# A two-layer hybrid decoder: the gate norm's root from ScalarE's table, first operands of a K block on VectorE, three sums ahead of the token sum

## Chip, core and metric

The kernel runs on one core of a Trainium2 chip. The metric is the device time of one execution in microseconds (us). The engines are called PE (TensorE, the matrix engine), DVE (VectorE), ACT (ScalarE), POOL (GpSimd) and SP (SyncE, which here issues the loads).

## What is computed

A trunk of two layers on 256 tokens of width 2048, in float32. Layer 0 mixes tokens by gated linear attention (GLA), layer 1 by attention with a forget gate (FoX); each mixer is followed by a gated MLP with a short convolution. Each half layer is normed and modulated by vectors that come from the condition c by one large product with w_mod.

```python
cond = jax.nn.silu(c)
for i in range(DEPTH):
    mod = (cond @ w_mod[i] + b_mod[i])[:, None, :]
    sh_m, sc_m, g_m, sh_f, sc_f, g_f = jnp.split(mod, 6, axis=-1)
    h = rmsnorm(x, norm_mix[i]) * (1.0 + sc_m) + sh_m
    ...                                   # gla_mixer or fox_mixer
    x = x + (1.0 + g_m) * y
    h = rmsnorm(x, norm_ffn[i]) * (1.0 + sc_f) + sh_f
    x = x + (1.0 + g_f) * conv_ffn(h, ...)
return rmsnorm(x, norm_final)

def gla_mixer(h, w_in, w_gate, b_gate, g_norm, w_out):
    q, k, v, r, a = split(h @ w_in)       # 1024, 1024, 2048, 2048, 16 columns
    ...                                   # chunked linear attention, 4 heads of 512
    o = rmsnorm(o, g_norm)                # for each head: the gate's norm
    return (o * silu(r)) @ w_out
```

## The kernel before

**Products.** Activations lie turned (128 features by 256 tokens), in 16 K tiles. Each float32 operand is split in a high and a low part: a weight tile `w` (128x1024, 512 KB) is cast by ACT to `wh` (L125), and DVE forms `wl` = w - wh (L129); the activation `h` has a high part from ACT (L528) and a low part from DVE (L533). A product takes three matmuls: high by high (L621), wh by the low part of h (L622), wl by the high part (L623). One weight tile against one K tile is 8 outputs by 3 matmuls of 128x256; such a step is a "use" of a weight.

**The start.** The scale and shift of the first four K tiles come from eight "early sums" on PE (L1270): eight tiles of w_mod of 1 MB, four matmuls each. ACT copies a finished row (`er`, L1276), PE turns it into columns (L1279) and DVE adds the bias (L1283). Ahead of them PE turns x (L441), and the token sum (L483) gives the norm's root. Between the later sums stand KEEP matmuls on a constant tile (L1308), whose output nobody reads.

**K blocks.** The rest of the modulation of layer 0 isn't there when the first weights are. So w_in is worked in three blocks of K tiles, 0 to 3, 4 to 8 and 9 to 15 (STARTS), and within each over the pieces q, k, v0, v1, r0, r1 (1024 columns each) and a (16). A piece's sums are copied out at the end of a block (L750) and put back into PSUM at the next (L609, `preload`). Meanwhile the w_mod products of the next block run on DVE as multiply-adds into `acc` (L273, L275; tiles `wm`), a certain number per use (`pace["bg"]`); at a column group's end DVE transposes and reduces (L285, L286), PE sums over quadrants (L302), and DVE adds the bias (L318). At a block's last use but one the queue is emptied (`drain_bg`), and at the block's start `h` for its first K tile is made (`hooks`). In `make_h` DVE multiplies x by the root (L527), ACT makes the high part (L528), then the scaled and shifted value is made again in float32, for K tiles 0 to 2 on DVE (L530), for others on ACT (L532), and DVE subtracts (L533).

**The gate's norm.** In the last block the attention runs as a side queue of steps, let out at `pace["side"]` steps per use. Its last steps: `apply` (per head; leaves the sums of squares in `pvar`, L916), `scale_of` (the reciprocal root `grs` for two heads by shift, constant and three Newton steps on DVE, L403 to L416), `normalise` (DVE puts a root on a diagonal `dg`, L422; PE spreads it, L424; DVE multiplies `oT`, L927), `open_gate` (silu on ACT, L942; product on DVE, L944). `raw_operand` then splits oT for w_out (L548, L549).

**Order.** The program is recorded in the order of the code and then put in order by a scheduler with a model of times; `tc.issue_after` pins an instruction behind another. DMA loads go out on SP's queue one after another (L248), and each waits there for its buffer.

## Time and profile before

| | |
|---|---|
| median of 3 runs | 2445.66 us (2445.61 to 2447.43) |
| the profiled execution | 2444.97 us, span 2443.3 us |
| mean granted PE clock | 0.989 |
| busy: PE, DVE, ACT, POOL | 98%, 78%, 54%, 1% of the span |
| DMA | 638.31 MB, 261 GB/s over the span |

Times in the rows of the profile are counted from the first instruction of the span. "[idle before <-releaser]" at a row's end is how long the engine did nothing ahead of it, and what ended that. A row with "x4" joins neighbours of one kind; "PEld" is the load of a stationary operand, which overlaps PE. The granted clock is 1.00 at full rate. A matmul's duration in a row is that of its way through the array, and the next one starts earlier.

### The profile page before, as it was taken

To read this page: it belongs to the slowest core of one execution; us is meant where nothing else is said; L and a number is where in the kernel's file an instruction comes from. 1 tells how busy PE (TensorE), PEld (TensorE's weight loads), DVE (VectorE), ACT (ScalarE), POOL (GpSimd) and SP (SyncE) were. 2 spreads that over 40 slices of the span, in tenths; PEclk is the share of its full clock that TensorE was granted. 3 is DMA by queue.
4 is the path that set the end of the run, shared out by engine and by line. 5 is a ranking of instruction groups with operands and counts; after the bars stand their busy time and mean duration, and the time that the engine had idled before them with its cause. 6 is when DMAs were issued, how large, how long until landed. Compare 5 with 4: busy or idle time off the path is not lost.

```text
span 2443.3 us, 46907 instructions
## 1 busy us (share of the span) xinstructions
PE 2388.1 (98%) x19089; PEld 2292.1 (94%) x19093; DVE 1901.7 (78%) x2548; ACT 1326.6 (54%) x1819; POOL 16.1 (1%) x35
## 2 busy tenths in 40 slices
PE   7999998999999999999999999999999999999998
PEld 5898898999999999999988888999999999999998
DVE  5887878887689999987577998887776777777544
ACT  4666864544656556543464555554755555555433
POOL 0000000000000000000000000000000000000000
PEclk9999998999999999999999999999999999999999
DMA  9997877899668999899589887686777777756553
GB/s 377 328 338 240 288 249 274 288 322 322 181 191 278 314 302 313 315 327 322 168 291 314 298 288 244 210 300 234 232 232 234 234 233 235 232 193 220 192 190 104
DMA packets 188293, 638.31 MB, mean 261 GB/s; under 512 B 23849, under 2 KB 24859, under 8 KB 187692
## 3 DMA queue, kind: packets, MB, share of 16 engines
q1 hardware_dynamic: 187112, 634.12, 77.2%
q8 instruction: 149, 2.44, 0.4%
q10 hardware_dynamic: 964, 1.20, 0.1%
q14 instruction: 68, 0.56, 0.1%
HBM read 633.14 MB, written 2.10 MB: 260 GB/s over the span
## 4 chain that ended last, share of the span: by engine, by line
PE 95%; DVE 2%; ACT 2%; DMA 1%; issue 1%; SPq 0%; DVEq 0%; ACTq 0%
PE pa L622 25%; PE pa L623 25%; PE pa L621 25%; PE pa L668 5%; PE pa L669 5%; PE pa L667 5%; DVE wl L129 1%; DMA wm<-in_w_mod_dram 1%; PE pe L1270 0%; DVE acc L275 0%; ACT wh L125 0%; PE pm L483 0%; PE pm L877 0%; DMA xtok<-in_x_dram 0%; PE pm L1088 0%
## 5 line engine op out<-in xcount | busy, mean ns | idle before, releaser
L125 ACT CAST wh<-w 128x1024 fp32r<-128x1024 f32 x820 | 857.4, 1048 | 965.7 <-PE pa L622 735.3
L129 DVE TENSOR_TENSOR wl<-w,wh 128x1024 fp32r<-128x1024 f32 x820 | 996.5, 1217 | 438.8 <-ACT wh L125 428.6
L622 PE MATMUL pa<-h,wh 128*128 128x256 f32 x3584 | 993.7, 278 | 13.3 <-DVE h L533 13.3
L621 PE MATMUL pa<-h,wh 128*128 128x256 f32 x3584 | 991.6, 278 | 2.2 <-ACT h L528 1.3
L623 PE MATMUL pa<-h,wl 128*128 128x256 f32 x3584 | 991.0, 278 | 1.7 <-DVE wl L129 1.7
L622 PEld LDWEIGHTS pa<-h,wh 128*128 128x128 f32 x3584 | 677.4, 189 | 15.1 <-DVE h L533 14.8
L621 PEld LDWEIGHTS pa<-h,wh 128*128 128x128 f32 x3584 | 675.3, 189 | 5.4 <-issue 1.5
L623 PEld LDWEIGHTS pa<-h,wl 128*128 128x128 f32 x3584 | 675.6, 189 | 2.0 <-DVE wl L129 1.9
L622 PE MATMUL pa<-op,wh 128*128 128x256 f32 x1920 | 529.4, 277 | 1.8 <-DVE op L549 1.8
L621 PE MATMUL pa<-op,wh 128*128 128x256 f32 x1920 | 528.9, 278 | 0.4 <-ACT op L548 0.2
L623 PE MATMUL pa<-op,wl 128*128 128x256 f32 x1920 | 524.8, 277 | 0.0
L275 DVE SCALAR_TENSOR_TENSOR acc<-wm,cT,acc 128x1024 f32<-128x1024 f32 (+2 forms) x360 | 444.3, 1235 | 10.7 <-DMA wm<-in_w_mod_dram 9.4
L622 PEld LDWEIGHTS pa<-op,wh 128*128 128x128 f32 x1920 | 362.0, 189 | 2.3 <-DVE op L549 2.3
L621 PEld LDWEIGHTS pa<-op,wh 128*128 128x128 f32 x1920 | 361.2, 189 | 1.1 <-ACT r L750 0.6
L623 PEld LDWEIGHTS pa<-op,wl 128*128 128x128 f32 x1920 | 359.2, 189 | 0.0
L668 PE MATMUL pa<-wh,h 128*128 128x512 f32 x512 | 200.2, 392 | 0.0
L667 PE MATMUL pa<-wh,h 128*128 128x512 f32 x512 | 198.8, 391 | 0.0
L669 PE MATMUL pa<-wl,h 128*128 128x512 f32 x512 | 194.4, 392 | 0.0
L669 PEld LDWEIGHTS pa<-wl,h 128*128 128x128 f32 x512 | 96.0, 188 | 19.7 <-DVE wl L129 0.3
L667 PEld LDWEIGHTS pa<-wh,h 128*128 128x128 f32 x512 | 96.1, 188 | 19.4
L668 PEld LDWEIGHTS pa<-wh,h 128*128 128x128 f32 x512 | 96.1, 188 | 19.2
L1140 ACT ACTIVATE y<-u,cw 128x256 f32<-128x256 f32 x176 | 101.6, 599 | 6.7 <-DVE act L1156 4.1
(264 smaller groups left out, 1351.3 us busy)
## 6 DMA issues: line engine op xcount, KB each, us to landing
wm<-in_w_mod_dram SPq DMA_DIRECT2D x320, 512.0 KB, 5.2
w<-in_ffn_w_up_dram SPq DMA_DIRECT2D x320, 512.0 KB, 4.5
w<-in_ffn_w_down_dram SPq DMA_DIRECT2D x176, 512.0 KB, 4.5
w<-in_fox_w_in_dram SPq DMA_DIRECT2D x128, 512.0 KB, 5.1
w<-in_gla_w_in_dram SPq DMA_DIRECT2D x96, 512.0 KB, 5.8
w<-in_gla_w_out_dram SPq DMA_DIRECT2D x32, 512.0 KB, 5.9
w<-in_ffn_w_up_dram SPq DMA_DIRECT2D x64, 256.0 KB, 4.0
w<-in_fox_w_out_dram SPq DMA_DIRECT2D x32, 512.0 KB, 5.9
```

The costliest lines, as they stand in the source:

```text
L125: nc.scalar.copy(out=hi, in_=src)
L129: order["v"] = nc.vector.tensor_tensor(out=lo, in0=src, in1=hi.bitcast(F32), op=ALU.subtract).ins
L275: nc.vector.scalar_tensor_tensor(out=st["a"], in0=wt[:, j, :], scalar=col, in1=st["a"], op0=ALU.mult, op1=ALU.add)
L621: nc.tensor.matmul(o, wh[:, ms], rh, start=(first and m % 2 == 0), stop=False, skip_group_check=True)
L622: nc.tensor.matmul(o, wh[:, ms], rl, start=False, stop=False, skip_group_check=True)
L623: nc.tensor.matmul(o, wl[:, ms], rh, start=False, stop=last, skip_group_check=True)
L667: nc.tensor.matmul(o, lh[:, ts_], wh[:, hs_], start=first, stop=False, skip_group_check=True)
L668: nc.tensor.matmul(o, ll[:, ts_], wh[:, hs_], start=False, stop=False, skip_group_check=True)
L669: nc.tensor.matmul(o, lh[:, ts_], wl[:, hs_], start=False, stop=last, skip_group_check=True)
L1140: nc.scalar.activation(y, u, AF.Identity, scale=cw[:, l * 3 + 2, r:r + 1], bias=cw[:, 6 + l, r:r + 1])
```

## The change

- `scale_of` uses `table_root`: DVE scales (L498 of the changed kernel), ACT takes the reciprocal root from its table (L506), and one third-order step on DVE mends it (L507 to L509). `scale_of(0)` runs before the end of piece v1, `scale_of(2)` before r0, and the norms of heads 2 and 3 go behind the first gate's steps. The pace of the side queue is 0.9 and then 1.2 steps a use for 0.8 and 1.4.
- In `make_h` the affine step for the first four K tiles of a block (of tiles 1 to 4 elsewhere) is on DVE. A new mark `fresh["h"]` makes the next use run `by_part`: all high by high products, then all with the low part, then all with wl. It is set when h of a block's first K tile is made.
- At the start three early sums stand ahead of the token sum (`first_sums`); KEEP is 3 for 5; the second weight's split is recorded ahead of h's second tile.
- `staged_h` queues the w_mod products for blocks 1 and 2 at once at the very start, at a pace worked out for each, and forces at a block's start only what that block needs; the hooks that make h sit one use earlier. Depth of prefetch and the constants SLOAD and NEAR of the loader change.

```diff
-SLOAD = 48
+SLOAD = 100
-NEAR = 20
+NEAR = 50
-KEEP = 5
+KEEP = 3
-GP0 = 0.8
-GP1 = 1.4
+GP0 = 0.9
+GP1 = 1.2
-EASE, N5 = 3, 5
+N5 = 5
+MARKS = (4, 9, 16)
+EASE = (4, 5)
+EARLY = 3
...
-        prefetch(PEND)
+        prefetch(min(PEND, fetched["use"] // 2 + 1))
...
-    def load_x(xs):
+    def load_x(xs, between):
...
         half_sum()
-        token_sum(ss["t"][:, 0, :], True, True)
+        with tc.issue_after(between()):
+            token_sum(ss["t"][:, 0, :], True, True)
...
+    def table_root(q, src, scale):
+        v = tmp.tile([P, 16], F32, tag="rs_v", name=nm("rv"))[:, :4]
+        nc.vector.tensor_scalar(out=v, in0=src, scalar1=scale, scalar2=None, op0=ALU.mult)
+        root_step(q, v, tmp.tile([P, 16], F32, tag="rs_t", name=nm("rt"))[:, :4])
+
     def token_rstd(q, n_):
-
-        order["r"] = nc.scalar.activation(q, ss["p"][:, :n_], AF.Abs_reciprocal_sqrt, bias=epsc).ins
-        t = t1("ra")[:, :n_]
-        nc.vector.scalar_tensor_tensor(out=t, in0=ss["p"][:, :n_], scalar=EPS, in1=q, op0=ALU.add, op1=ALU.mult)
+        root_step(q, ss["p"][:, :n_], t1("ra")[:, :n_])
+
+    def root_step(q, src, t):
+
+        order["r"] = nc.scalar.activation(q, src, AF.Abs_reciprocal_sqrt, bias=epsc).ins
+        nc.vector.scalar_tensor_tensor(out=t, in0=src, scalar=EPS, in1=q, op0=ALU.add, op1=ALU.mult)
         nc.vector.scalar_tensor_tensor(out=t, in0=t, scalar=-0.5, in1=q, op0=ALU.mult, op1=ALU.mult)
         nc.vector.scalar_tensor_tensor(out=q, in0=t, scalar=1.5, in1=q, op0=ALU.add, op1=ALU.mult)
 
@@ -526,11 +539,23 @@
...
-            if m < 3:
-                nc.vector.tensor_scalar(out=t, in0=t, scalar1=sc, scalar2=sh, op0=ALU.mult, op1=ALU.add)
-            else:
-                nc.scalar.activation(t, t, AF.Identity, scale=sc, bias=sh)
+            with ExitStack() as es:
+                if m == 1 and order["w"] is not None:
+                    es.enter_context(tc.issue_after(order["w"]))
+                    order["w"] = None
+                if m - (max(b for b in STARTS if b <= m) if (l, kind) == (0, "m") else 1) < 4:
+                    nc.vector.tensor_scalar(out=t, in0=t, scalar1=sc, scalar2=sh, op0=ALU.mult, op1=ALU.add)
+                else:
+                    nc.scalar.activation(t, t, AF.Identity, scale=sc, bias=sh)
             ins = nc.vector.tensor_tensor(out=lo, in0=t, in1=hi.bitcast(F32), op=ALU.subtract).ins
+            if m == 0 and (l, kind) == (0, "m"):
+                with tc.issue_after(ins):
+                    split_to(1, 2)
+                    with tc.issue_after(hot):
+                        split_to(2, 2)
+                order["w"] = order["v"]
+            if m == 0 or (l, kind) == (0, "m") and m in STARTS:
+                fresh["h"] = True
...
+        def mms(m, k, wh, wl, rh, rl, n_=None):
             first, last = base is None and k == kts[0], k == kts[-1]
             ms = slice(m * P, (m + 1) * P)
             o = ps[m // 2][:, m % 2, :]
-            nc.tensor.matmul(o, wh[:, ms], rh, start=(first and m % 2 == 0), stop=False, skip_group_check=True)
-            nc.tensor.matmul(o, wh[:, ms], rl, start=False, stop=False, skip_group_check=True)
-            nc.tensor.matmul(o, wl[:, ms], rh, start=False, stop=last, skip_group_check=True)
+            for i, (w_, r_) in enumerate(((wh, rh), (wh, rl), (wl, rh))):
+                if n_ is None or n_ == i:
+                    mm = nc.tensor.matmul(o, w_[:, ms], r_, start=(first and i == 0 and m % 2 == 0),
+                                          stop=last and i == 2, skip_group_check=True)
+            return mm.ins
+
+        def by_part(ms, args):
+            edge = None
+            for n_ in range(3):
+                with ExitStack() as es:
+                    if edge is not None:
+                        es.enter_context(tc.issue_after(edge))
+                    for m in ms:
+                        last_ = mms(m, *args, n_)
+                    edge = last_
...
-                for args in held if k == kts[1] else ():
+                if k == kts[1] and fresh["h"]:
+                    fresh["h"] = False
+                    by_part(range(4), held[0])
                     for m in range(4):
-                        mms(m, *args)
+                        mms(m, *held[1])
+                elif k == kts[1]:
+                    for args in held:
+                        for m in range(4):
+                            mms(m, *args)
                 while k == kts[1] and held:
                     args = held.pop(0)
                     for m in range(4, 8):
                         mms(m, *args)
+            elif fresh["h"]:
+                fresh["h"] = False
+                by_part(range(8), (k, wh, wl, rh, rl))
...
-            return lambda: rsqrt(grs[:, 2 * hd:2 * hd + 4], pvar[:, 2 * hd:2 * hd + 4], 1.0 / 512.0, 4)
+            return lambda: table_root(grs[:, 2 * hd:2 * hd + 4], pvar[:, 2 * hd:2 * hd + 4], 1.0 / 512.0)
...
-        side.extend((apply(0), scores(2), apply(1), scores(3)))
+        side.extend((apply(0), scores(2), apply(1), scores(3), scale_of(0)))
         fold("v1", piece("v1", kts, off["v1"]))
         drain_side()
-        side.extend((apply(2), apply(3), scale_of(0), scale_of(2), normalise(0), normalise(1), normalise(2), normalise(3)))
+        side.extend((apply(2), apply(3), normalise(0), normalise(1), scale_of(2)))
         pace["side"], pace["sacc"] = GP0, 0.0
...
         side.extend(open_gate(0, b) for b in range(4))
+        side.extend((normalise(2), normalise(3)))
...
+    def first_sums():
+        with tc.issue_after(order["x"]):
+            for args in todo[:EARLY]:
+                last_ = early_sum(*args)
+        return last_
+
+    load_x(xs, first_sums)
     with tc.issue_after(order["s"]):
         turn_rows()
     first_h = make_h(0, "m")
     for i, args in enumerate(todo):
         if i + WIDE < len(todo):
             early_load(*todo[i + WIDE])
+        if i < EARLY:
+            continue
...
+    need = {}
+
     def staged_h(m):
-        if m in STARTS[:-2]:
-            n_ = STARTS.index(m) + 1
-            for key in ("sc_m", "sh_m"):
-                queue(mod_tasks(0, key, STARTS[n_] * P, BLOCKS[n_] * P, wide=True))
-            n_use = 6 * BLOCKS[n_ - 1]
-            set_pace(n_use - EASE)
-            end = fetched["use"] + n_use + (m > 0)
-            hooks[end - 1] = drain_bg
-            hooks[end] = lambda: h(STARTS[n_])
+        if m == 0:
+            for m0, m1 in zip(MARKS, MARKS[1:]):
+                for key in ("sc_m", "sh_m"):
+                    queue(mod_tasks(0, key, m0 * P, (m1 - m0) * P, wide=True))
+                need[m0] = len(bg)
+            pace["bg"] = need[MARKS[0]] / float(6 * BLOCKS[0] - EASE[0])
+            hooks[6 * MARKS[0] - 1] = lambda: h(MARKS[0])
+            hooks[6 * MARKS[1]] = lambda: h(MARKS[1])
+        elif m == MARKS[0]:
+            pace["bg"], pace["acc"] = len(bg + pending) / float(6 * BLOCKS[1] - EASE[1]), 0.0
+        if m in need:
+            while steps_done[0] < need[m]:
+                bg_step()
+            flush_resting(True)
         return first_h(m)
 
-    h = lazy(staged_h, KT, 2, STARTS)
+    h = lazy(staged_h, KT, 2, MARKS)
```

How the order of instructions moves, at three places. PE at the start, from behind the turning of x, before (wm are tiles of w_mod, ss the squares summed over tokens, rows and brow small vectors that are turned):

```order
L483 MATMUL pm_219<-ss_153,onesD 128x256
L206 MATMUL pm_221<-ident,rows_106 128x98
L1270 MATMUL pe_237<-wm_139,cz_120 32x512 x4
L1270 MATMUL pe_237<-wm_141,cz_120 32x512 x4
L1270 MATMUL pe_237<-wm_143,cz_120 32x512 x4
L1270 MATMUL pe_237<-wm_145,cz_120 32x512 x3
L211 MATMUL pm_225<-ident,brow_127 128x96
L1270 MATMUL pe_237<-wm_145,cz_120 32x512
L1270 MATMUL pe_269<-wm_235,cz_120 32x512 x3
```

and after:

```order
L1318 MATMUL pe_219<-wm_139,cz_120 32x512 x4
L1318 MATMUL pe_219<-wm_141,cz_120 32x512 x4
L1318 MATMUL pe_219<-wm_143,cz_120 32x512 x4
L489 MATMUL pm_232<-ss_153,onesD 128x256
L209 MATMUL pm_234<-ident,rows_106 128x98
L1318 MATMUL pe_219<-wm_145,cz_120 32x512 x4
L214 MATMUL pm_238<-ident,brow_127 128x96
L1327 MATMUL pm_262<-ones,er_260 128x1 x4
L1318 MATMUL pe_269<-wm_248,cz_120 32x512 x4
```

Three sums moved ahead of the token sum (L483 before, L489 after), and the first row's turn (L1327) stands ahead of the fifth sum.

ACT at the start of block 1 (h is the operand of K tile 4 and on, r the last piece's sums that are copied out, w the weight tiles), before:

```order
L125 CAST wh_1064<-w_987 128x1024
L125 CAST wh_1100<-w_989 128x1024
L125 CAST wh_1152<-w_991 128x1024
L528 ACTIVATE h_1128<-hn_1129,mod 128x256
L528 ACTIVATE h_1128<-hn_1134,mod 128x256
L528 ACTIVATE h_1128<-hn_1139,mod 128x256
L750 COPY r_197_1144<-pa_980 128x512
L750 COPY r_197_1144<-pa_981 128x512
L750 COPY r_197_1144<-pa_982 128x512
L750 COPY r_197_1144<-pa_983 128x512
L528 ACTIVATE h_1128<-hn_1191,mod 128x256
L125 CAST wh_1181<-w_993 128x1024
```

and after:

```order
L128 CAST wh_994<-w_941 128x1024
L128 CAST wh_1026<-w_991 128x176
L541 ACTIVATE h_1097<-hn_1098,mod 128x256
L541 ACTIVATE h_1097<-hn_1103,mod 128x256
L541 ACTIVATE h_1097<-hn_1108,mod 128x256
L797 COPY r_199_1145<-pa_987 128x512
L797 COPY r_199_1145<-pa_988 128x512
L128 CAST wh_1065<-w_1024 128x1024
L797 COPY r_199_1145<-pa_989 128x512
L797 COPY r_199_1145<-pa_990 128x512
L541 ACTIVATE h_1097<-hn_1188,mod 128x256
L128 CAST wh_1115<-w_1063 128x1024
```

Before, the casts of the block's first weights (wh_1064 and wh_1100 for its first pair) stood ahead of the operands; after, the pair's casts (wh_1065 and wh_1115) stand behind the operands and behind two and four of the copies. The affine steps of these K tiles, on ACT behind the last row before (L532), are on DVE (L547).

DVE in block 2 from the root of heads 2 and 3 on (rv, rt and grs are the root's tiles of 128x4; th is the gate's silu, op the operand of w_out), before:

```order
L403 TENSOR_SCALAR rv_3529<-pvar 128x4
L129 TENSOR_TENSOR wl_3813<-w_3577,wh_3812 128x1024
L275 SCALAR_TENSOR_TENSOR acc_3700<-wm_3698,cT,acc_3700 128x1024
L944 TENSOR_TENSOR oT_2783<-oT_2783,th_3772 128x512
L944 TENSOR_TENSOR oT_2783<-oT_2783,th_3807 128x512
L405 TENSOR_SCALAR grs<-rv_3529 128x4
L129 TENSOR_TENSOR wl_3847<-w_3629,wh_3846 128x1024
L927 TENSOR_TENSOR oT_2783<-oT_2783,pm_3636 128x1024
L275 SCALAR_TENSOR_TENSOR acc_3700<-wm_3740,cT,acc_3700 128x1024
L407 TENSOR_SCALAR grs<-grs 128x4
```

and after:

```order
L498 TENSOR_SCALAR rv_3564<-pvar 128x4
L132 TENSOR_TENSOR wl_3781<-w_3571,wh_3780 128x1024
L278 SCALAR_TENSOR_TENSOR acc_3681<-wm_3679,cT,acc_3681 128x1024
L991 TENSOR_TENSOR oT_2777<-oT_2777,th_3622 128x512
L991 TENSOR_TENSOR oT_2777<-oT_2777,th_3683 128x512
L507 SCALAR_TENSOR_TENSOR rt_3566<-rv_3564,grs 128x4
L132 TENSOR_TENSOR wl_3820<-w_3615,wh_3819 128x1024
L974 TENSOR_TENSOR oT_2777<-oT_2777,pm_3523 128x1024
L278 SCALAR_TENSOR_TENSOR acc_3681<-wm_3716,cT,acc_3681 128x1024
L508 SCALAR_TENSOR_TENSOR rt_3566<-rt_3566,grs 128x4
```

The places between large instructions are the same; in the last row the chain is at its third instruction of 13 before, and at its third of four after, with the table's root on ACT between the first two.

More of the change, by code (lines that the diff above doesn't have):

```diff
@@ L94 @@
     cnt = [0]
-    order = {"v": None, "f": None}
+    order = {"v": None, "f": None, "w": None}
     def nm(s):
@@ L343 @@
     pending = deque()
+    steps_done = [0]
     def prefetch(depth):
@@ L353, in bg_step @@
         if pending:
+            steps_done[0] += 1
             pending.popleft()()
@@ L440, in load_x @@
                 for tt in range(TT):
-                    nc.tensor.transpose(px[:, j * T + tt * P:j * T + (tt + 1) * P],
-                                        xs[tt][:, (m + j) * P:(m + j + 1) * P], ident)
+                    order["x"] = nc.tensor.transpose(px[:, j * T + tt * P:j * T + (tt + 1) * P],
+                                                     xs[tt][:, (m + j) * P:(m + j + 1) * P], ident).ins
             nc.scalar.copy(out=xT[:, m:m + 2, :], in_=px.rearrange("p (j t) -> p j t", j=2))
@@ L554 @@
     plan = []
+    fresh = {"h": False}
     def plan_stream(w, kts, cols, moving=False):
@@ L615, in stream_a @@
         preload([p.rearrange("p j t -> p (j t)") for p in ps], base)
-        def mms(m, k, wh, wl, rh, rl):
+        def mms(m, k, wh, wl, rh, rl, n_=None):
             first, last = base is None and k == kts[0], k == kts[-1]
@@ L1292 @@
         early_load(*args)
-    load_x(xs)
+    def first_sums():
[4 more added lines that the diff above has]
+    load_x(xs, first_sums)
     with tc.issue_after(order["s"]):
```

## Prediction

> **What bounds the kernel now.** I read the shares of busy time first, then TensorE's (PE's) waits, then short windows with the granted clock, then the timeline at the places that those two name. The shares (busy us, share of the span, instructions):
>
> ```profile
> PE 2388.1 (98%) x19089; PEld 2292.1 (94%) x19093; DVE 1901.7 (78%) x2548; ACT 1326.6 (54%) x1819; POOL 16.1 (1%) x35
> ```
>
> PE works for 98% of the span, and the change leaves the number of its large products as it is. So a gain can only come out of what PE waits, or out of time in which it works at half clock. Its waits (total us, times, longest):
>
> ```profile
> PE pa L622 <- DVE h L533: 13.3, 7, 5.4
> PE pm L424 <- DVE dg L422: 8.3, 1, 8.3
> PE pm L483 <- DVE ss L476: 4.0, 1, 4.0
> PE pa L623 <- DVE wl L129: 1.7, 1, 1.7
> PE pm L306 <- ACT pm L310: 1.2, 1, 1.2
> ```
>
> Five windows of PE alone (us, busy and instructions, granted clock, DMA share, GB/s):
>
> ```profile
> 210.50:214.50 4.00, 4.00 (x24) 0.58 0.42 128
> 204.30:206.50 2.20, 2.20 (x13) 0.50 0.45 67
> 117.30:122.10 4.80, 4.80 (x24) 0.50 1.02 374
> 392.00:405.50 13.50, 11.24 (x48) 0.50 0.26 98
> 42.00:47.30 5.30, 5.21 (x24) 0.50 1.02 405
> ```
>
> Each of these windows follows a wait of PE, and in it PE runs at half clock. 24 products in 4.80 us are 0.200 us each; in the row of 361 to 384 us below, at clock 1.00, 189 in 21.67 are 0.115. So cold work loses 43% of its time. At 0.58 a window is cold for 0.42/0.50 of it, 3.4 of 4.00 us. That makes losses of 1.4, 0.9, 2.1, 4.8 and 2.2 us beside the waits themselves. The change touches four places: the start, the starts of K blocks 1 and 2, and the gate's norm.
>
> **The start (A).** Timeline rows (start, duration, engine, line, out<-in, count, idle before and its releaser), and the row of the DMA list with the median us to landing:
>
> ```profile
> 2.19 17.25 SPq L248 DMA_DIRECT2D wm<-in_w_mod_dram  x8
> wm<-in_w_mod_dram SPq DMA_DIRECT2D x8, 1024.0 KB, 11.2
> 34.56 1.06 PE L1270 MATMUL pe<-wm,cz 128*32 128x512 f32 x8
> 35.70 0.59 ACT L1276 COPY er<-pe 128x512 f32<-128x512 f32 x1 [8.03 <-PE pe L1270]
> 37.43 0.16 DVE L1283 TENSOR_TENSOR mod<-pm,bm 128x4 f32<-128x4 f32 x1 [4.81 <-PE pm L1279]
> 38.72 0.74 PE L621 MATMUL pa<-h,wh 128*128 128x256 f32 x4 [1.34 <-ACT h L528]
> 42.09 0.58 PE L623 MATMUL pa<-h,wl 128*128 128x256 f32 x1 [1.71 <-DVE wl L129]
> ```
>
> Before, PE stands 4.0 us before the token sum, then does all eight early sums, so that the eighth starts at 34.56 although its tile, issued by 19.44, has landed at about 19.44 + 11.2 = 30.7. After, three sums fill the hole ahead of the token sum, and each later sum is followed by 3 fill products and not 5. The last sum then starts with its tile, at about 31.0, and ends at 32.1. From there the rows of before repeat: copy 0.59, turn 1.05, the addition 0.16, and the first operand, 4.16 us from the sum's start to the first product in before (38.72 - 34.56). That gives 35.2, 3.5 us earlier. The 1.71 us before the first low-weight product go too: the new order does eight products with the high part of h, eight with its low part and only then eight with wl, and wl's subtraction stands right behind the first low part on VectorE (DVE); I count 1.2 of it, since some of ACT's casts and operands still stand ahead of wl. The cold stretch of 2.2 us I leave as it is, since fewer fills leave more idle time ahead of it. A = 4.7 us; its bounds are 2.2 (weights, issued after the eighth sum's tile, land later than I take and keep the casts back by 2.5) and 6.9 (warm).
>
> **Block 1 (B).** Timeline:
>
> ```profile
> 109.67 0.68 DVE L318 TENSOR_TENSOR mod<-pm,bm 32x5 f32<-32x5 f32 x4 [0.66 <-PE pm L302]
> 110.39 1.58 ACT L528 ACTIVATE h<-hn,mod 128x256 fp32r<-128x256 f32 x3
> 111.88 2.02 ACT L750 COPY r<-pa 128x512 f32<-128x512 f32 x4
> 114.28 1.04 ACT L125 CAST wh<-w 128x1024 fp32r<-128x1024 f32 x1
> 115.36 1.23 DVE L129 TENSOR_TENSOR wl<-w,wh 128x1024 fp32r<-128x1024 f32 x1 [3.19 <-ACT wh L125]
> 116.50 1.09 DVE L533 TENSOR_TENSOR h<-hn,h 128x256 fp32r<-128x256 f32 x3
> 116.97 0.58 PE L622 MATMUL pa<-h,wh 128*128 128x256 f32 x1 [5.42 <-DVE h L533]
> ```
>
> Read as a chain: the addition, three operands, four copies of the last piece, the cast of a weight that is not yet wanted, its wl, and only then the low part that PE waits 5.42 us for. After, the scale and shift that feed the low parts lie on DVE, and the low part stands ahead of wl. But the first weight's cast, done long before in the old order, now stands on ACT behind the operands and two of the copies, and the new order by parts is not spent here: the operand is now prepared one step earlier, and the mark that asks for this order is taken by the last K tile of piece r1. Counted from the end of r1 (109.3): addition done at 1.0, operands at 2.5, two copies at 3.5, cast 4.5, low part ready by then, wl 5.7 to 6.2. So PE has its pair complete at about 115.5 and not at 117.0, with four products done ahead of it and not two: 1.4 + 0.2, and some 0.4 less cold time. B = 2.0 us; from 0.5 (copies and cast as late as before, which the first three rows would give) to 4 (the whole of wl's place gained, 1.23, and the cold 2.1).
>
> **Block 2 (C).**
>
> ```profile
> 202.00 1.11 DVE L286 TENSOR_REDUCE red<-mt 128x16 f32<-128x512 f32 x2
> 203.16 0.41 PE L302 MATMUL pm<-red,quad 128*128 128x28 f32 x2 [1.68 <-DVE red L286]
> 209.88 0.39 PE L622 MATMUL pa<-h,wh 128*128 128x256 f32 x1 [2.78 <-DVE h L533]
> ```
>
> Here the reduction itself is late, and the same chain follows. After, the last reduction stands some 3 us ahead of r1's end, and three wl of the block stand ahead of its start on DVE. What is left from r1's end: addition at 1.0, copies and operands 2.55, low part 3.5; PE has 16 small products of its own meanwhile, and I work out 0.6 + 0.75 us of idle time, shorter, each, than any wait that a cold window follows in these rows. C = 1.68 + 2.78 + 0.9 + 1.4 - 1.35 = 5.4; from 3.1 (both cold stretches stay) to 6.8 (no idle time).
>
> **The gate's norm (D).** The first row is of the view of one source line (ns min/median/max, first and last start):
>
> ```profile
> L403 DVE TENSOR_SCALAR rv<-pvar x2: 162/166/170, 329.9 to 354.5; 128x4 f32<-128x4 f32 x2
> 345.53 1.28 ACT L942 ACT_TABLE_LOAD   x1
> 345.00:361.00 16.00, 15.78 (x136) 15.33 (x134) 12.78 (x19) 11.33 (x17) 0.00 (x0) 1.00 0.72 227
> 361.00:384.00 23.00, 21.67 (x189) 21.41 (x188) 22.38 (x29) 12.13 (x16) 0.00 (x0) 1.00 0.88 306
> 380.10 1.28 DVE L275 SCALAR_TENSOR_TENSOR acc<-wm,cT,acc 128x1024 f32<-128x1024 f32 x1
> 382.44 0.15 DVE L411 TENSOR_TENSOR rt<-rt,grs 128x4 f32<-128x4 f32 x1
> 391.81 0.15 DVE L416 SCALAR_TENSOR_TENSOR grs<-rt,grs 128x4 f32<-128x4 f32 x1
> 392.34 0.80 PE L424 MATMUL pm<-dg,ones 128*128 128x128 f32 x2 [8.26 <-DVE dg L422]
> 394.46 1.22 DVE L927 TENSOR_TENSOR oT<-oT,pm 128x1024 f32<-128x1024 f32 x1 [0.99 <-PE pm L424]
> 398.79 1.28 DVE L549 TENSOR_TENSOR op<-oT,op 128x512 fp32r<-128x512 f32 x2
> ```
>
> The root of heads 2 and 3 is a chain of 13 small instructions on DVE, 354.5 to 391.8. Each takes 0.15 us, but stands between a wl (1.2) and a sum of the modulation (1.28), so that the chain advances by 37.3/12 = 3.1 us a step. In the window 361 to 384 (columns PE, weight loads, DVE, ACT) DVE is busy for 22.38 of 23.00 us and ACT for 12.13. After, four of the chain are left on DVE and one is on ACT. Between the first, at about 355 as before, and dg the order has ten large DVE instructions (1.2 to 1.3), six half ones (0.64) and three small: 17 us, less the overlap of about 0.08 that the rows of neighbours show for each (a row's start is earlier than the end of the one before): dg at about 370. PE comes to its broadcast some 98 products earlier than before, 384.1 (392.34 - 8.26) less 98 x 0.115, so 373, so this wait goes. Next late are the normalised products and the low part of the out projection's K tile 8: from dg on I count 15.6 us, 386.0, against 385.1 for PE. D = 8.26 + 1.2 (the wait at L306) + 4.8 of cold - 0.9 = 13.4; at most 14.3 without the new wait, at least 6.6, rival 1.
>
> Against it: ACT must load its table three times more here, 3 x 1.28 = 3.8 us, and while it waits for DVE's scaling it holds up a cast. ACT has 10.9 us idle in the window, and a cast that comes 0.7 us later still stands a whole step ahead of its products. I cost it at nothing; without that cover it is 3.8 us.
> The Trainium skill, "ScalarE: Activation LUTs", section "What ACT_TABLE_LOAD costs", counts about 2.7 us for each switch, 1.4 of it a drain, and advises to group calls by table; it speaks against this change, and by it three loads would be 8.0 us. The trace has 1.28 us and no idle time before the load, so by 8.0 us ACT's idle 10.9 would still hold it.
>
> **What costs nothing.** The constants for loads keep the order on SP's queue nearly as it was (one tile of w goes ahead of one of wm). At the starts of the feed-forward nets two affine steps move from ACT to DVE; their products are not first in the block, and those ahead of them hide them: 0, from -1 to +1 (a wait as long as one DVE step).
>
> **Sum.** 4.7 + 2.0 + 5.4 + 13.4 = 25.5 us. The profiled execution took 2444.97 us (span 2443.3, and 1.7 around it), the median of the runs is 2445.66, 0.7 more. 2445.0 - 25.5 = 2419.5, and 2420.2 as a median.
>
> **Rivals.**
> 1. DVE becomes the limit at the gate. It has 0.6 us free in the 23 above, and it must take on, ahead of K tile 8, two normalisations (1.22), four half products and four half low parts (0.64): 7.6 us, less nine small steps (1.4) and the free 0.6, so 5.6 us too much, unless the slower side queue (1.2 steps a use for 1.4) spreads these or fewer sums stand between; I counted three sums from dg on. PE then waits 5.6 us at tile 8 and runs cold for one stretch like those of the blocks (2.1 lost at 117.3), less the 0.9 already counted: D = 13.4 - 6.8 = 6.6, time 2427. The full window speaks for it; against it, 12.78 of 16 us are DVE's share in the stretch before, where the first two heads now go. Chance 0.2.
> 2. The change doesn't do what it says at the blocks: the order by parts is spent on r1, and the starts still wait for copies, cast and wl. B and C are nothing: 2427.6. For it speaks that misplaced mark; against it, the earlier reduction. Chance 0.12; with rival 1 together, 2434.4, 0.03.
> 3. The loads become the limit, and the kernel is slower. After no longer empties the queue of wm at the block starts, and loads of 896 KB stand before weights. The DMA view of 31 to 212 us has
>
> ```profile
> GB/s 403 396 406 402 405 397 404 402 400 404 401 382 365 237 184 166 231 273 407 385 216 177 353 417 333 315 417 410 382 381 391 228 358 375 327 336 170 51 190 84
> DMA packets 19959, 58.64 MB, mean 324 GB/s; under 512 B 3665, under 2 KB 3665, under 8 KB 19943
> ```
>
> These 58.6 MB must be there 12.1 us (A, B and C) earlier than in those 181, which asks 347 GB/s. The whole gain is gone when they take 25.5 us longer than that, so below 58.6/194.4 = 302 GB/s; at 290 they take 202 us and the time is 2453. Slices with work for the queues show about 400. Chance 0.03.
> 4. The clock is kinder: the start of block 0 is warm and A is 6.9: 2418.0. The waits of 1.68 and 1.71 us in the rows above are followed by 0.50, which speaks against it. Chance 0.1.
> The Trainium skill, "TensorE: Matmul & The Clock Gate", "Part 1: The HAM clock gate", has the clock halved only after an idle window of about 3.4 us; by that rule this start would be warm. The trace differs: 1.68 us were enough.
>
> **How the numbers follow.** My forecast as summed has 0.5, the rivals 0.48; the rest is open. A change under 0.2% (4.9 us) can't be told from none by such a measurement. All bounds at their good ends give 2445.7 - 33 = 2412.7 (6.9, 4, 6.8, 14.3 and 1); rivals 1 and 2 give 2427 to 2428, with a few us of A or B missing 2432, and only both together or rival 3 lie above. So 2412 to 2432. Faster 0.93, same 0.03, slower 0.04.
>
> **What would show it.** The profile after should have no wait of PE for dg over 1 us, first products at about 35, starts of blocks 1 and 2 at 0.50 for some 4 us and for none, and a clock of 1.00 from 385 on. A wait at low parts near 385 shows rival 1; waits for wl or h of over 4 us at both block starts show rival 2; waits for w from DMA near 100 or 190 show rival 3. I would be wrong above all if the later part of the kernel, which I take as untouched, shifts by some us because its loads start at other times.

## The result, and the profile after

| | before | after |
|---|---|---|
| median of the runs (4 each) | 2446.41 us (2445.61 to 2447.43) | 2426.19 us (2422.12 to 2427.81) |
| ratio after to before | | 0.9915, 95% interval 0.9897 to 0.9932 |
| profiled execution, span | 2444.97 us, 2443.3 us | 2425.23 us, 2423.5 us |

The change is worth about 20 us by the medians. The same program, run again beside the last experiments, took 2426.43 us, ratio 0.9924 (0.9907 to 0.9942). Shares of busy time and PE's waits of the changed kernel (total us, times, longest):

```profile
PE 2380.0 (98%) x19083; PEld 2283.5 (94%) x19087; DVE 1903.6 (79%) x2545; ACT 1318.3 (54%) x1809; POOL 16.1 (1%) x35
PE pa L649 <- DVE h L550: 5.7, 4, 2.6
PE pm L489 <- DVE ss L482: 4.6, 2, 3.5
PE pa L649 <- ACT wh L128: 4.1, 3, 3.4
PE pe L1318 <- DMA wm<-in_w_mod_dram: 2.8, 2, 2.2
PE pa L649 <- DVE op L574: 0.8, 1, 0.8
```

The wait for dg of 8.3 us is gone from the list, and so is most of the 13.3 us for the low part of h. New are 3.4 us for a cast, 2.2 for a tile of w_mod, and a wait of 3.5 us for ss, the sum of squares ahead of the first feed-forward net.

PE does the same 18,048 large products in both kernels, in nearly the same order, so the start of the n-th of them in the one trace less that in the other tells where time is won and lost. The marks below are the same products in every row; "net" is what follows up to the next mark. Kernel before minus kernel after, in us:

| from product to product | place | after | after, again | forecast |
|---|---|---|---|---|
| start to 48 | the start (A) | +4.62 | +4.15 | +4.7 |
| 48 to 432 | rest of block 0 | -1.90 | -1.89 | 0 |
| 432 to 528 | start of block 1 (B) | +2.05 | +1.48 | +2.0 |
| 528 to 936 | rest of block 1 | -1.45 | -1.44 | 0 |
| 936 to 1152 | start of block 2 (C) | +6.20 | +6.21 | +5.4 |
| 1152 to 2640 | block 2 and out projection (D) | +16.11 | +16.21 | +13.4 |
| 2640 to 9000 | into and through the first feed-forward net | -5.87 | -3.95 | 0 |
| 9000 to the end | the rest | -0.03 | -0.08 | 0 |

Four gains came about in about the forecast sizes, and then 4 to 6 us are lost at one place that the forecast costed at nothing. That place in the timeline of the changed kernel, first DVE and then PE:

```profile
439.16 1.22 DVE L132 TENSOR_TENSOR wl<-w,wh 128x1024 fp32r<-128x1024 f32 x1
440.30 1.28 DVE L278 SCALAR_TENSOR_TENSOR acc<-wm,cT,acc 128x1024 f32<-128x1024 f32 x1
441.49 2.44 DVE L747 SCALAR_TENSOR_TENSOR xT<-pa,mod,xT 128x256 f32<-128x256 f32 x6
445.95 0.43 DVE L482 TENSOR_TENSOR ss<-ss 128x256 f32<-128x256 f32 x1
446.43 0.70 PE L489 MATMUL pm<-ss,onesD 128*128 128x256 f32 x2 [3.50 <-DVE ss L482]
```

DVE still does a sum of the modulation at 440.3, so that the six additions to x behind it start in one go at 441.5, when PE has but 1.4 us of products left; the squares' sum is ready 3.5 us after PE's last product. Why DVE is late, the windows show (us, then busy us and instructions of PE, weight loads, DVE, ACT, POOL, clock, DMA share, GB/s), the first four rows of before and the last four of after:

```profile
354.00:384.00 30.00, 28.45 (x245) 27.75 (x243) 29.38 (x39) 16.53 (x22) 0.00 (x0) 1.00 0.88 300
384.00:400.00 16.00, 5.82 (x23) 4.86 (x23) 12.35 (x21) 4.83 (x19) 0.00 (x0) 0.64 0.73 287
400.00:425.00 25.00, 25.00 (x199) 25.00 (x199) 19.07 (x25) 11.65 (x27) 0.00 (x0) 0.89 0.68 231
425.00:467.00 42.00, 42.00 (x373) 42.00 (x372) 38.12 (x42) 18.55 (x20) 0.00 (x0) 1.00 0.97 339
...
345.00:361.00 16.00, 15.08 (x127) 14.44 (x127) 16.00 (x22) 14.27 (x33) 0.00 (x0) 1.00 0.83 252
361.00:384.00 23.00, 22.88 (x200) 22.68 (x199) 23.00 (x30) 11.24 (x15) 0.00 (x0) 1.00 0.88 303
384.00:400.00 16.00, 16.00 (x144) 16.00 (x143) 14.48 (x15) 5.81 (x6) 0.00 (x0) 1.00 0.99 361
400.00:442.00 42.00, 42.00 (x372) 41.96 (x371) 40.37 (x45) 18.52 (x34) 0.00 (x0) 1.00 0.97 365
```

Between the root of heads 2 and 3 and the end of the out projection DVE is busy 93.9 us of 97 in the changed kernel. In before the same piece of the program (354 to 467) left it 14 us idle out of 113, 9.6 of them between 384 and 425 us, in the old wait for dg and behind it.

The order on DVE has changed here too. In the changed kernel the half sum of the squares (L482, at 445.95) stands behind all eight additions to x; in before it (L476, at 467.47) stands ahead of the last two and ends 0.5 us before PE's last product of the out projection:

```profile
467.47 0.41 DVE L476 TENSOR_TENSOR ss<-ss 128x256 f32<-128x256 f32 x1
468.47 0.88 DVE L700 SCALAR_TENSOR_TENSOR xT<-pa,mod,xT 128x256 f32<-128x256 f32 x2 [0.58 <-PE pa L623]
```

From that product to the first of the feed-forward net 11.1 us pass in the changed kernel and 5.7 in before.

### The profile page after: what moved, and what is told of

It is laid out like the page before. It is cut to its first block, busy times and chain, and to the rows that moved or that the text cites. A ratio compares the mean times of both kernels' runs of the same rounds, so it can differ in the third digit from the quotient of the medians.

```text
span 2423.5 us, 46891 instructions
## 1 busy us (share of the span) xinstructions
PE 2380.0 (98%) x19083; PEld 2283.5 (94%) x19087; DVE 1903.6 (79%) x2545; ACT 1318.3 (54%) x1809; POOL 16.1 (1%) x35
## 4 chain that ended last, share of the span: by engine, by line
PE 93%; DVE 3%; DMA 2%; ACT 1%; issue 1%; SPq 0%; DVEq 0%; ACTq 0%
PE pa L649 74%; PE pa L715 5%; PE pa L714 5%; PE pa L716 5%; DMA wm<-in_w_mod_dram 2%; DVE wl L132 1%; DVE acc L278 1%; PE pt L298 0%; PE pm L489 0%; ACT wh L128 0%; PE pm L924 0%; PE pm L1136 0%; PE pm L946 0%; PE pm L1082 0%; PE pm L1100 0%
## 5 line engine op out<-in xcount | busy, mean ns | idle before, releaser
L649 PE MATMUL pa<-h,wh 128*128 128x256 f32 x7168 | 1229.7, 278 | 12.3 <-DVE h L550 5.7
L649 PEld LDWEIGHTS pa<-h,wh 128*128 128x128 f32 x7168 | 1078.8, 189 | 16.9 <-DVE h L550 6.7
L649 PE MATMUL pa<-h,wl 128*128 128x256 f32 x3584 | 975.9, 278 | 0.6 <-DVE wl L132 0.4
L649 PEld LDWEIGHTS pa<-h,wl 128*128 128x128 f32 x3584 | 667.2, 188 | 2.3 <-DVE wl L132 1.5
L649 PE MATMUL pa<-op,wh 128*128 128x256 f32 x3840 | 653.5, 277 | 1.0 <-DVE op L574 0.8
L649 PEld LDWEIGHTS pa<-op,wh 128*128 128x128 f32 x3840 | 575.5, 188 | 1.7 <-DVE op L574 1.3
L1191 DVE SCALAR_TENSOR_TENSOR y<-u,cw,y 128x254 f32<-128x254 f32 x176 | 83.2, 479 | 2.8
L1189 DVE SCALAR_TENSOR_TENSOR y<-u,cw,y 128x255 f32<-128x255 f32 x176 | 84.1, 478 | 0.0
L1210 ACT COPY u<-pa 128x512 f32<-128x512 f32 x88 | 49.8, 582 | 0.7
L541 ACT ACTIVATE h<-hn,mod 128x256 fp32r<-128x256 f32 x64 | 35.4, 596 | 11.6 <-DVE mod L321 8.4
```

The lines of the kernel that those rows point to most:

```text
L541: hot = nc.scalar.activation(hi, t, AF.Identity, scale=sc, bias=sh).ins
L649: mm = nc.tensor.matmul(o, w_[:, ms], r_, start=(first and i == 0 and m % 2 == 0), stop=last and i == 2, skip_group_check=True)
L1189: nc.vector.scalar_tensor_tensor(out=y[:, 1:], in0=u[:, :T - 1], scalar=cw[:, l * 3 + 1, r:r + 1], in1=y[:, 1:], op0=ALU.mult, op1=ALU.add)
L1191: nc.vector.scalar_tensor_tensor(out=y[:, 2:], in0=u[:, :T - 2], scalar=cw[:, l * 3, r:r + 1], in1=y[:, 2:], op0=ALU.mult, op1=ALU.add)
L1210: nc.scalar.copy(out=u[:, 2 * b:2 * b + 2, :], in_=ps[b])
```

## The experiments

The reading to be tested: from block 2's second half to the first feed-forward net the sum of DVE's work sets a floor, and what PE no longer waits at the gate it waits at the net. The rivals: ScalarE's table loads and squares are late; the feed-forward net's own start is at fault; or other parts of the change lose the time. Beside it, some other parts of the change were undone. The order of the modulation's sums (`staged_h`), to which B and C belong, was not. The ratios below are to runs of the kernel before on the same chip.

**The gate norm's part alone, on the kernel before.**

```diff
-            return lambda: rsqrt(grs[...], pvar[...], 1.0 / 512.0, 4)
+            return lambda: table_root(grs[...], pvar[...], 1.0 / 512.0)
...
-        side.extend((apply(0), scores(2), apply(1), scores(3)))
+        side.extend((apply(0), scores(2), apply(1), scores(3), scale_of(0)))
...
-        side.extend((apply(2), apply(3), scale_of(0), scale_of(2), normalise(0), normalise(1), normalise(2), normalise(3)))
+        side.extend((apply(2), apply(3), normalise(0), normalise(1), scale_of(2)))
...
+        side.extend((normalise(2), normalise(3)))
...
-GP0 = 0.8
-GP1 = 1.4
+GP0 = 0.9
+GP1 = 1.2
```

> The kernel before with the gate norm's part of the change alone (table root, order of the side queue, its paces). Theory: the wait of 8.3 us and the cold stretch behind it go (16 to 17 us up to the out projection), and VectorE, now full up to the first feed-forward net, gives some 6 back there: 10 to 11 us faster than before, 2435 to 2436. Rival (the loss ahead of the first net comes from other parts of the change): 15 to 17 us faster, 2430.

Measured 2436.66 us, ratio 0.9958 (0.9943 to 0.9973), 10.5 us by the medians. From product 1152 to 2640 it gains 16.83 us, and from there to 9000 it loses 6.94. In a window of 330 to 480 us its waits are

```profile
PE pm L492 <- DVE ss L485: 3.4, 1, 3.4
PE pa L631 <- DVE h L542: 2.3, 1, 2.3
PE pa L631 <- DVE op L558: 0.8, 1, 0.8
```

So the loss comes with the gate's part and needs none of the others. (The wait for h is not new: before has one of 2.2 us at 482.9.)

**The old root at the new place.**

```diff
-            return lambda: table_root(grs[...], pvar[...], 1.0 / 512.0)
+            return lambda: rsqrt(grs[...], pvar[...], 1.0 / 512.0, 4)
```

> The changed kernel with the old root (13 small VectorE instructions, no table) at the new place of the step and with the new order of the side queue. Theory of the prediction (the chain advances by one small instruction per 3 us): the root of heads 2 and 3 would be ready about 37 us after 345.5, at about 382, PE wants it at about 370: a wait of some 8 to 10 us comes back with its cold stretch, but VectorE catches up in it, so that the wait of 3.5 us before the first feed-forward net goes; 2430 to 2434. Rival (the order of the side queue alone was worth the gain): no wait for dg over 2 us, 2426.

Measured 2433.21 us, ratio 0.9945 (0.9930 to 0.9959). The same window:

```profile
PE pm L429 <- DVE dg L427: 8.9, 2, 8.1
PE pa L649 <- DVE h L550: 2.3, 1, 2.3
```

The wait for dg is back at its old size, and the wait of 3.5 us for ss and the loss behind it are gone (-0.02 from 2640 to 9000). Taking the chain from 13 to four instructions on DVE is what removes the wait; the new order of the side queue alone doesn't. By the medians this kernel is 7 us slower than the changed one, and the gate norm's part alone is 10.5 us faster than the kernel before, and not the 16 to 17 that the gate itself gains.

**Less work for DVE in that stretch.**

```diff
+                        n_ = 64 if (l, key, f0) == (0, "sh_f", 0) and k % 2 else width
-                        nc.vector.scalar_tensor_tensor(out=st["a"], in0=wt[:, j, :], ...)
+                        nc.vector.scalar_tensor_tensor(out=st["a"][:, :n_], in0=wt[:, j, :n_], ...)
```

> The changed kernel, but 8 of the 16 multiply-adds of the second modulation half that run during the out projection (sh_f of layer 0) work on 64 columns instead of 1024, which leaves out that part of the modulation: about 9 us less work for VectorE between the gate's norm and the first feed-forward net. Theory (VectorE is full from 341 to 446 us, so that the work which the old 8 us wait had covered now ends after the out projection): the wait of PE for ss at 442.9 (3.50 us) goes and the cold stretch behind it too, the first feed-forward product comes 25 us ahead of the kernel before and not 20; time 5 to 6 us below the changed kernel, 2420 to 2421. Rival 1 (the squares or the table loads of ScalarE are late there): wait stays, no change beyond 1 us. Rival 2 (it is the start of the feed-forward net itself, affine steps on VectorE): the wait for ss may go, but the products still start 20 us ahead.

Measured 2422.02 us, ratio 0.9898 (0.9884 to 0.9913), 4.2 us below the changed kernel by the medians; the intervals overlap. DVE has 6.0 us less in the last window (34.35 for 40.37, where 9 had been expected), with PE and ACT much as in the changed kernel:

```profile
400.00:442.00 42.00, 42.00 (x373) 42.00 (x372) 34.35 (x47) 19.51 (x36) 0.00 (x0) 1.00 1.01 386
PE pm L490 <- DVE ss L483: 3.0, 2, 1.8
439.74 0.88 DVE L748 SCALAR_TENSOR_TENSOR xT<-pa,mod,xT 128x256 f32<-128x256 f32 x2 [2.35 <-PE pa L650]
```

The wait for ss is 1.8 us for 3.5 (the other of the two is at the start), and from 2640 to 9000 it loses 0.45 us for 5.87 and 3.95. The net's first product comes 23.3 us ahead of the kernel before, for 20.1 and 20.8 in the changed kernel; 25 had been expected. For the half that went, rivals 1 and 2 fall: neither ACT's work nor the net's start was touched. The other half isn't DVE's load: in the last row DVE stands 2.35 us before its first addition to x. What is left is the order. In the 14 traces of this case the half sum stands ahead of the last two additions in the five without this wait, and behind all eight in the nine with it, this one among them. No run changed that order alone, so its share isn't measured.

**The same work, moved.** First, earlier sums; second, the gate's products on GpSimd; third, sums away from both the gate and the out projection (on top of the two edits below).

```diff
-BG0, BG1 = 0.95, 0.75
+BG0, BG1 = 1.15, 0.75
```

> The changed kernel with the modulation's sums of block 2 at a pace of 1.15 a use for 0.95 up to piece v1, where VectorE had about 30 us idle (205 to 345 us); some four to five sums leave the out projection's stretch. Nothing is left out. Theory (VectorE full): the wait for ss ahead of the first feed-forward net shrinks by 3 to 5 us, to about none, and the time comes to 2421 to 2423. Rival (ScalarE late, or the start of the net): 2426 as the changed kernel. A second risk: pieces q to v1 of block 2 get waits for wl, worth 1 to 3 us.

```diff
-                nc.vector.tensor_tensor(out=o, in0=o, in1=th, op=ALU.mult)
+                nc.gpsimd.tensor_tensor(out=o, in0=o, in1=th, op=ALU.mult)
```

> The changed kernel with the gate's products (oT times silu, eight of 0.64 us) on GpSimd and not on VectorE. Theory (VectorE's sum of work from 341 to 446 us sets the loss ahead of the first feed-forward net): 5 us of work less, the wait for ss falls from 3.5 to under 1 us and the cold stretch goes, 2421 to 2422. Rival: GpSimd takes 2 us or more for each, or slows VectorE, and the low parts of the out projection's operand come late: new waits for op of 2 to 5 us at 350 to 375 us, 2426 to 2430.

```diff
-BG0, BG1 = 0.95, 0.75
+BG0, BG1 = 1.3, 0.5
```

> As the run with the tied mark and five fills, with the modulation's pace at 1.3 a use up to v1 and 0.5 in r0 and r1: three to seven sums leave the stretch from 341 us to the first feed-forward net for the one where VectorE had 30 us idle, and unlike the run at 1.15 none is added where the gate's steps run. Theory (VectorE's work between the gate and the first net): no wait for ss, no new wait for op over 1 us; 3 to 5 us below its sister, 2414 to 2417. Rival (the wait goes only to another place): within 2 us of its sister.

Measured 2425.47, 2425.98 and 2424.32 us (ratios 0.9914, 0.9920, 0.9913): none is clear of the changed kernel. In each the wait for ss is gone and another stands in its place. PE's new waits in the window of 330 to 480 us, in the order of the three:

```profile
PE pa L649 <- DVE op L574: 2.7, 1, 2.7
PE pa L649 <- ACT op L573: 2.0, 1, 2.0
...
PE pa L649 <- DVE wl L132: 2.7, 2, 2.1
PE pm L429 <- DVE dg L427: 1.2, 1, 1.2
...
PE pa L649 <- ACT op L573: 2.5, 1, 2.5
PE pm L429 <- DVE dg L427: 2.1, 1, 2.1
```

The theory failed in all three, and the third's rival came true. The second didn't relieve DVE: GpSimd took 1.74 to 2.41 us for a product of 0.68 on DVE, and a multiply-add on DVE took up to 2.31 us meanwhile, for 1.28. One window of all engines, of the changed kernel and of the three:

```profile
341.00:446.00 105.00, 100.89 (x877) 99.81 (x876) 101.81 (x123) 56.52 (x95) 0.00 (x0) 1.00 0.92 323
...
341.00:446.00 105.00, 100.33 (x865) 99.94 (x864) 92.12 (x111) 57.52 (x83) 0.00 (x0) 0.97 0.85 294
...
341.00:446.00 105.00, 99.90 (x856) 98.86 (x855) 102.02 (x106) 54.54 (x91) 17.04 (x8) 0.98 0.87 308
...
341.00:446.00 105.00, 99.48 (x845) 98.69 (x843) 89.27 (x106) 55.21 (x81) 0.00 (x0) 0.97 0.81 281
```

In the first and the third DVE is idle for 13 and 16 us of the 105, and still nothing is gained. So the sum of DVE's work isn't the floor by itself; when its steps come counts as well. The attention's last step on ACT (L955) ends at 342.0 and 343.8 us there, for 336.5 in the changed kernel, and the gate's steps come late behind it. That the earlier sums hold it back is my reading and wasn't tested alone.

From product 1152 to 9000, in which both the gate and the net lie, the net gains are: after 10.24 and 12.25, these three 10.43, 11.36 and 8.07, the gate's part alone 9.89, and less work 15.65. The five other kernels with the same work there, told of below, stand between 11.00 and 14.41. Moving work gained nothing that could be told from this spread. Taking work away lies above all of it, but by 1.2 us only, where two executions of the changed kernel differ by 2.0.

**The start without sums ahead.**

```diff
-EARLY = 3
+EARLY = 0
...
-        with tc.issue_after(between()):
-            token_sum(ss["t"][:, 0, :], True, True)
+        token_sum(ss["t"][:, 0, :], True, True)
```

> The changed kernel with all eight early sums behind the token sum again (three fills as there). Theory (the three sums fill a hole and nothing else waits for them): the hole of 4 us comes back, the eighth sum is done about 1.5 us later, since it still waits for its tile at 33 us and the sums behind the hole catch up in part; 2426 to 2428. Rival (the landing of the last tile sets the start alone): no change, 2425 to 2426.

Measured 2422.40 us, ratio 0.9905 (0.9890 to 0.9921), not slower than the changed kernel. At product 48 it is 4.72 us ahead of the kernel before, as the changed kernel is (4.62 and 4.15). Its start, the changed kernel's behind it, and last a row of the changed kernel run again:

```profile
20.28 1.19 PE L488 MATMUL pm<-ss,onesD 128*128 128x256 f32 x2 [3.96 <-DVE ss L481]
33.53 1.07 PE L1317 MATMUL pe<-wm,cz 128*32 128x512 f32 x8
37.24 3.63 PE L648 MATMUL pa<-h,wh 128*128 128x256 f32 x16 [0.89 <-ACT h L540]
...
30.32 1.55 PE L1318 MATMUL pe<-wm,cz 128*32 128x512 f32 x8 [2.23 <-DMA wm<-in_w_mod_dram]
33.19 1.53 PE L1318 MATMUL pe<-wm,cz 128*32 128x512 f32 x8
37.37 3.61 PE L649 MATMUL pa<-h,wh 128*128 128x256 f32 x16 [0.89 <-ACT h L541]
40.77 1.22 PE L649 MATMUL pa<-h,wl 128*128 128x256 f32 x8
...
32.90 1.06 PE L1318 MATMUL pe<-wm,cz 128*32 128x512 f32 x8 [0.89 <-DMA wm<-in_w_mod_dram]
```

The hole of 4 us is back, and the first product comes at the same time. The time lies below both expectations, and the rival's reason isn't the one either: here no sum waits for a tile, and PE comes to the eighth at 33.53 by its own row of sums and fills. In the changed kernel PE waits 2.23 us for the seventh tile and, run again, 0.89 us for the eighth. By the semaphores in the traces the eighth tile is there at 31.4 us here and at 33.0 and 32.9 in the changed kernel; why it comes later there is open. So PE's own row and the tile's landing end at nearly the same time. With three fills the three sums ahead of the token sum are worth nothing that these runs show.

**Five fills for three** (`KEEP`), **the mark tied to its K tile** (`fresh["h"]` holds the K tile and only that tile's use, or its pair, takes it), **and both.**

```diff
-KEEP = 3
+KEEP = 5
...
-            elif fresh["h"]:
-                fresh["h"] = False
+            elif fresh["h"] == k:
+                fresh["h"] = None
```

> The changed kernel with five fill products and not three behind each late early sum. The trace of the changed kernel has the clock at 0.60 from 30 to 34 us and 0.54 from 37.3 to 41. Theory (short idle pieces of 1 to 2 us halve the clock for the next 3.4 us): two more fills of 0.22 us don't close a wait of 2.2 us for the seventh tile, so the start stays cold, 2425 to 2427. Rival (three fills were too few): the first 24 products are warm, 1.6 us less and the first product 0.5 us earlier, 2424.

> The changed kernel with the mark for the order by parts tied to the K tile whose operand is new, so that blocks 1 and 2 start by parts and the last tile of piece r1 doesn't. My reading (at block 1 PE waits for wh, which stands ahead of either order; at block 2 wl is done before): under 1 us, 2425 to 2426. Rival (the misplaced mark cost the two block starts): 2 to 4 us less, 2422 to 2424.

> The changed kernel with the mark tied to its K tile and with five fills. If both gains of their own runs hold (5 and 6 us by their medians, of which the trace shows 1 to 2 each by a cause, the rest at the first feed-forward net): 2418 to 2420. If most of them was chance at the start and at the clock: 2421 to 2425.

Measured 2419.92 us (ratio 0.9897, 0.9882 to 0.9912), 2420.91 (0.9902, 0.9885 to 0.9918) and, both together, 2424.74 (0.9914, 0.9898 to 0.9929). They don't add up, and the intervals of all three overlap the changed kernel's; I don't call any of them faster. By the traces neither acts as the rivals would have it: at product 48 the kernel with five fills is 4.48 us ahead (4.62 without), and from 48 to 1152 the tied mark gains 4.92 (4.91 without). With five fills the rest of block 0 loses nothing (-0.04 for -1.90), but the first wait of block 1 is 4.33 us for 3.37; through product 1152 it is 11.13 us ahead, the changed kernel in its two executions 9.53 and 8.51. The wait of 3.5 us for ss stands in all three, and from 2640 to 9000 they lose 5.26, 2.29 and 4.19 us.

**More weights loaded ahead** at block 1.

```diff
-NEAR = 50
+NEAR = 20
```

> The changed kernel with the loader's constant NEAR back at 20, so that from use 20 on six weights are loaded ahead and not two. In the order ScalarE then casts the first three weights of block 1 ahead of the block's operands, as in the kernel before. Theory (the wait of 3.4 us for wh at 109.3 in the changed kernel comes from the weight that is loaded late, which puts the cast behind two copies): that wait goes and with it most of the cold stretch, 4 to 5 us; 2421 to 2422. Rival (the operands and the additions set that start): the wait moves to the low part of h, at most 1 us is gained, 2425. Risk: the modulation's tiles load later, and the reduction ahead of block 1 or 2 is late by 1 to 3 us.

Measured 2421.96 us, ratio 0.9902 (0.9888 to 0.9917), the time that I expected, but not for my reason. Waits of 100 to 130 us, this kernel's and then the changed one's:

```profile
PE pa L649 <- ACT pa L635: 4.3, 1, 4.3
PE pa L649 <- ACT h L541: 1.6, 1, 1.6
...
PE pa L649 <- ACT wh L128: 3.4, 1, 3.4
```

The wait for wh is gone, and a longer one for the sums put back into PSUM has taken its place, which now stand behind the casts in ACT's queue. Block 1 starts 4.9 us worse (-2.85 for +2.05 from 432 to 528). It is made up at block 2 (+7.85 for +6.20 from 936 to 1152), in the rest of block 1 and in D. This expectation left out what ACT must do at that start besides the casts; the cause of the later gains is not settled.

## Why the prediction came out as it did

The forecast was 2420.2 us, and 2426.2 was measured: within the range, faster as said, with a gain of 20 us for 25.5.

- **A, the start: the sum right, its make-up wrong.** The step that failed is "the last sum then starts with its tile, at about 31.0". It starts at 33.19 in the changed kernel, behind the seventh sum, whose tile came at 30.3, and three fills at a clock of 0.60 (again: at 32.90, with its own tile), and the first product is 1.4 (again: 2.1) us earlier and not 3.5. The sums ahead of the token sum bring nothing. The rest of the 4.6 us comes behind the first product: 48 products take 7.2 us from it on (37.37 to 44.58; again: 8.4), and 10.5 in before. In the row at 40.77 the first products with wl follow at once, where before PE had waited 1.71 us; that fits the order by parts and the earlier split, which weren't undone. That the sum is met to 0.1 us is luck: with the changed start product 48 is 4.5 to 6.0 us ahead in the other kernels, and with the start of before (the gate's part alone) it was 1.75 us behind.
- **B, the start of block 1: right** (2.1 and 1.5 for 2.0; 0.6 to 2.3 in four other kernels with the same code up to there), with the wait for the cast behind operands and copies that the working named.
- **C, the start of block 2: right in kind by the rows, 0.8 us too small.** It wasn't undone alone.
- **D, the gate: right in mechanism and too small by 2.7.** DVE makes dg at 361.06 us, which is 370.0 on the clock of before (the shift there is 9.0); the walk through the order gave 370. No product waits for the low part of K tile 8, where I had set 0.9. Two waits for op behind the broadcast in before, 0.17 and 0.52 us at 397.8 and 399.5, were not in the sum and are gone, and one at 362.5 fell from 1.33 to 0.80. That leaves some 0.6 us by which the cold stretch cost more than the 4.8 taken. ACT's table loads took 1.28 us each, and PE has no wait behind them.
- **The rest of blocks 0 and 1: a term that was left out**, 3.3 us in all. ACT's waits show where it may come from, of 39 to 214 us in before, of 37 to 212 after:

```profile
ACT wh L125 <- PE pa L622: 35.4, 24, 3.2
...
ACT v L797 <- PE pa L716: 19.3, 4, 6.2
ACT wh L128 <- DMA w<-in_gla_w_in_dram: 13.6, 11, 3.2
ACT h L541 <- DVE mod L321: 8.4, 1, 8.4
```

Before, ACT's casts ran ahead of PE until their buffers were full. After, they stand in ACT's queue behind copies that wait for a piece's end, and behind the operands of block 1, 8.4 us. Where a cast then comes, wl and PE are late by tenths of a us. With six weights ahead the loss in the rest of block 1 is gone (0.00 for -1.45) and that in block 0 stays (-1.89); with five fills both are nearly gone, and with five fills and the tied mark the one in block 1 is back (-1.97). So more than one thing orders these casts, and which is open.
- **The feed-forward net: the step that failed most.** "What costs nothing" has it at 0, from -1 to +1; it is -5.9 (again: -4.0), outside those bounds. I looked there at the affine steps alone. Rival 1 had the mechanism, a full DVE, and had even the row for it (22.38 of 23.00 us), but asked for its effect at K tile 8 only. There DVE is just in time; the work that didn't fit was carried for 60 us more and came out at the next point at which PE needs DVE's last result. By the run with less work that is about half of the wait of 3.5 us; the other half stays with DVE idle ahead of it, and goes with the changed order of the half sum, whose share is open.
- **The later part** of the kernel doesn't move: -0.03 us from product 9000 on, against the doubt at the end of the prediction.
- Rival 2 had no part in it: the mark was misplaced as read, and tying it changed nothing at the block starts. Rival 3: ACT waited for weights by DMA, 13.6 us in 11 times, which before doesn't show; PE's own loss of 3.3 us in those blocks is all that can have come of it. Rival 4: the start is cold in part (0.54 from 37.3 to 41), as the rows of before had it.

## What to carry to other kernels

When a wait of the bound engine is removed, ask what another engine did in that time: here DVE had 14 us of spare time in 113, most of it in and behind PE's wait, and a quarter to two fifths of the gain at the gate was lost again 70 us later. Sum the second engine's work over the whole stretch to the next point where everything it has done is needed, and compare it with the stretch as it will be; a check of the next operand alone isn't enough. The sum isn't enough either. Moved work left DVE 13 and 16 us idle and gained nothing, because other steps came late; and with 6 us of work left out half of the wait stayed, with DVE idle ahead of it. So look also at the order in which the second engine makes the result that is needed next.

## What the runs showed of the hardware

The same wait of 3.50 us ahead of the first feed-forward net is followed by different clocks in different runs. PE alone in three windows, of the changed kernel run again, the changed kernel, and the one with five fills:

```profile
446.00:450.00 4.00, 2.61 (x14) 1.00 0.84 235
...
446.00:450.00 4.00, 3.57 (x10) 0.65 0.50 174
...
446.00:450.00 4.00, 4.00 (x10) 0.50 0.38 135
450.00:454.00 4.00, 3.76 (x18) 0.50 0.00 0
454.00:458.00 4.00, 4.00 (x15) 0.50 0.00 0
```

In the first the clock stays at 1.00 behind the wait, in the last it is 0.50 for 12 us, although PE is busy by its rows. The Trainium skill, "TensorE: Matmul & The Clock Gate", "Part 1: The HAM clock gate", has the full clock back after one busy window of about 3.4 us; the last rows differ, with 0.50 over three such windows. In the middle one of these, 450 to 454 us, PE does 16 products of a single column (L298). From PE's last product of the out projection to the net's first 9.4, 11.1 and 15.1 us pass in the three. Not all of it is lost: the kernel with five fills is 16.9 us ahead of the kernel before at the net's first product and 22.1 at product 9000. So the clock is one reason why single executions differ; that it accounts for the 5.7 us between the fastest and the slowest run of the changed kernel wasn't tried. And GpSimd is no help for the gate's products: one of 128x512, 0.68 us on DVE, took 1.74 to 2.41 us there.
